# A hybrid attention and recurrence block on one core: buffers of the recurrence moved out of the merge's memory, score matmuls reshaped, and stores moved to GpSimd

## The chip, the cores and the metric

The kernel runs on one core of one Trainium2 chip, in one launch. The core has a matrix engine (TensorE, PE), a vector engine (VectorE, DVE), an activation engine (ScalarE, ACT), a general engine (GpSimd, POOL) and an engine that mostly issues transfers (SyncE, SP). Each engine works through its own instructions in order, and waits at an instruction for semaphores that other engines and transfers raise. The metric is the device time of one execution in microseconds (us); lower is better. Everything is computed in fp32.

## The reference

The input x is 1024 positions by 1024 channels. It is normalised, and one input projection gives everything that two branches need. Branch A is dilated window attention with three groups of eight heads; branch B is a gated linear recurrence in both directions with eight heads.

```python
ATTN_GROUPS = ((128, 1), (512, 4), (2048, 16))     # (window, dilation)
...
def dilated_window_attention(q, k, v, bias_table, window, dilation):
    side = (window // 2) // dilation
    blk = side
...
    s = jnp.einsum('bnqrhd,bnkrhd->bnrhqk', qb, kh) + bias
    s = jnp.where(valid[None, :, None, None], s, NEG_INF)
    m = jnp.max(s, axis=-1, keepdims=True)
    p = jnp.exp(s - m)
...
def hgrn2_scan(q, i, z_f, lb):
    f = lb + (1.0 - lb) * jax.nn.sigmoid(z_f)
    return gla_chunk_scan(q, 1.0 - f, i, jnp.log(f))
```

A block of 64 queries sees the keys of its own block and of the block on each side (its halo), as far as these exist; keys outside the window or the sequence are masked. The three groups' outputs are merged per head, weighted by their softmax denominators. In the recurrence, the logarithms of the gate f are summed along each chunk, and q and k are scaled by exponentials of those sums. Each branch is multiplied by its gate and projected; the two are merged by sigmoid gates, pass an output projection and are added to x.

## The kernel before, in words

The work runs in stages, told here by the profiled run's times. Until about 684 us PE does the largest products of the input projection (each fp32 product as three products of high and low parts: tiles whi, wlo, hh, hl). From 684 to 850 comes attention, with the products for the recurrence's values (psum tiles gp) filling PE between attention's steps. From 850 to 925 the groups' outputs are merged (tiles og, macc, gal), beside products for the recurrence's q and f. From 925 to 1233 comes the recurrence, and then the end projections.

The order of instructions isn't written by hand. A planner (classes Plan and Builder) keeps a model clock for each engine; tasks have dependencies and a priority, and `tick` and `burst` place them when the model says that their inputs are there and the buffers are free. Matmuls of attention are placed between units of gp products. `Ring` is a set of buffers used in turn: a buffer is handed out again once its last use is done. All instructions are recorded by one helper at line 58, so that tiles name them.

Attention handles a pair of blocks of 128 positions at a time, for four heads (a pair is given by group g, half hv and first block i0). `scores` (from line 1340) puts query times key into psum tiles sc, two for each block (j = 0, 1). In group 0, a block u takes 4 matmuls of 128 keys, the block's own, and then small ones of 64 queries by 64 keys for the halos (`halo(g, i)`): keys to the left for the first 64 queries (e = 0), keys to the right for the other 64 (e = 1). The halos share columns 128 to 191. At the two ends of the sequence there is no halo on one side; that corner (64 partitions by 2 x 64) is set to NEG by a memset on DVE ahead of the matmuls. In group 1 a block takes 4 matmuls of 192 keys; in group 2 only matmuls of 64 by 64. Behind the matmuls DVE adds the bias and takes the maximum of each row (`as<-sc,abias`), ACT exponentiates (`as<-as,neg`), PE transposes (pT), DVE and ACT copy out (apt), and `pv` multiplies by the values (o); DVE and ACT copy one half each of the result into one of two buffers aos, and `keep_o` (line 1490) stores it to DRAM, oD, by SP. `evac_early` (line 1640) copies a finished gp product into a buffer `stage` and stores it to ibD, by SP too, through `store` (line 653).

SBUF is given out in pools that open and close. The merge's pool "merge" closes when the merge's last store (oaD<-macc) is placed, and pool "hgrn2" opens on the same memory, so whatever first writes a tile of "hgrn2" waits for the merge's last users of that memory. Pool "hgrn" had been opened earlier, on other memory. The recurrence's first head goes: sigmoid of sk and logarithm qr<-sk on ACT (`logs`), the running sum Bc on DVE (`sums`), copies mm on POOL, differences qr and q_0 on DVE, exponentials km, qr and q on ACT, decays G (`decay`), then sk times G on DVE and the transposes kT on PE. Before, all of these tiles but sk lie in "hgrn2".

## Time and profile before

| | |
|---|---|
| times of three runs | 1441.4, 1436.46, 1439.83 us |
| median | 1439.83 us |
| the profiled execution's own time | 1438.22 us |
| its span, first to last instruction | 1436.4 us |
| mean granted clock of TensorE | 0.996 |
| TensorE busy | 1416.6 us, 99% of the span |
| VectorE, ScalarE, GpSimd busy | 67%, 61%, 24% |

A row of the timeline gives start, duration, engine, line, operation, output<-inputs, shapes, and how many like it stand in a row; in brackets is the idle time of the engine just before it and what ended it. A row on PE in which many matmuls stand together counts each matmul in two records. PEclk is the granted clock as a share of full speed. "SPq" and "POOLq" are transfers issued by those engines.

### The profile page before, as it was taken

The numbers are of one execution on the slowest core, as the hardware profiler recorded it, in microseconds if no ns is written. First come the engines' busy times: TensorE is split into PE (matmuls) and PEld (weight loads), VectorE is DVE, ScalarE is ACT, GpSimd is POOL, SyncE is SP. The second block draws the span as 40 slices with busy tenths as digits, with TensorE's granted clock in tenths as the row PEclk, the third lists the DMA queues.
The fourth block names the chain that finished last, engine by engine and source line by source line (L and its number), as shares of the span: only waits on it lengthen the run. The fifth ranks groups of instructions, "written<-read, shape, count | busy, mean of one in ns | idle before, by whom it ended". The sixth has DMA issues, their size and how long they took to land. (4 is left out here: it accounts for less than half of the span.)

```text
span 1436.4 us, 24409 instructions
## 1 busy us (share of the span) xinstructions
PE 1416.6 (99%) x8666; PEld 1177.1 (82%) x8666; DVE 962.4 (67%) x1935; ACT 875.2 (61%) x1879; POOL 338.4 (24%) x340
## 2 busy tenths in 40 slices
PE   9999999999999999999899999989999999999998
PEld 7788888888888888888778788878888888787887
DVE  6673677778675788431356657886888786358973
ACT  7743667566574766444577643576878684558461
POOL 0102334455433433334020000031222221001011
PEclk9999999999999999999999999999999999999999
DMA  7856567776733354423887329755444453778665
GB/s 239 183 140 193 169 200 168 186 160 154 173 118 104 80 119 113 129 104 118 273 280 245 118 71 273 212 122 125 116 105 127 103 153 84 226 227 218 186 162 137
DMA packets 231862, 230.32 MB, mean 160 GB/s; under 512 B 74755, under 2 KB 157979, under 8 KB 231228
## 3 DMA queue, kind: packets, MB, share of 16 engines
q1 hardware_dynamic: 217052, 203.41, 46.7%
q0 software_dynamic: 13824, 25.17, 11.5%
q8 instruction: 68, 1.11, 0.3%
q14 instruction: 54, 0.44, 0.1%
q10 hardware_dynamic: 864, 0.19, 0.1%
HBM read 168.77 MB, written 81.43 MB: 174 GB/s over the span
## 5 line engine op out<-in xcount | busy, mean ns | idle before, releaser
L58 POOL TENSOR_TENSOR wlo<-qraw,whi 128x512 fp32r<-128x512 f32 x135 | 194.2, 1444 | 378.1 <-ACT whi L58 287.8
L58 ACT ACTIVATE whi<-qraw 128x512 fp32r<-128x512 f32 x189 | 117.5, 626 | 100.9 <-DVE qraw L58 42.5
L58 DVE TENSOR_TENSOR qraw<-qraw,qraw 128x512 f32<-128x512 f32 x108 | 96.3, 892 | 40.5 <-POOL wlo L58 25.3
L58 PE MATMUL gp<-hh,whi 128*128 128x512 f32 x264 | 109.5, 415 | 0.0
L58 PE MATMUL gp<-hh,wlo 128*128 128x512 f32 x264 | 103.7, 393 | 0.0
L58 PE MATMUL gp<-hl,whi 128*128 128x512 f32 x264 | 103.1, 390 | 0.0
L58 ACT ACTIVATE whi<-raw 128x512 fp32r<-128x512 f32 x92 | 57.6, 627 | 60.4 <-DMA raw<-in_w_in_dram 31.6
L58 ACT ACTIVATE as<-as,neg 128x192 f32<-128x192 f32 (+1 forms) x192 | 77.7, 408 | 21.5 <-DVE neg L58 21.5
L58 PE MATMUL qA<-hh,whi 128*128 128x512 f32 x216 | 84.0, 389 | 0.0
L58 PE MATMUL qA<-hl,whi 128*128 128x512 f32 x216 | 84.0, 389 | 0.0
L58 PE MATMUL qA<-hh,wlo 128*128 128x512 f32 x216 | 84.0, 389 | 0.0
L58 POOL COPY mm<-Bc 128x8 f32<-128x8 f32 x64 | 32.6, 541 | 204.3 <-DVE Bc L58 126.0
L58 PE MATMUL gp<-whi,hh 128*128 128x512 f32 x192 | 79.1, 412 | 1.0 <-ACT stage L58 1.0
L58 PE MATMUL gp<-wlo,hh 128*128 128x512 f32 x192 | 75.2, 392 | 0.4 <-DVE wlo L58 0.4
L58 PE MATMUL gp<-whi,hl 128*128 128x512 f32 x192 | 75.1, 391 | 0.0
L58 DVE TENSOR_TENSOR wlo<-qraw,whi 128x512 fp32r<-128x512 f32 x54 | 37.3, 691 | 51.6 <-ACT whi L58 50.9
L58 ACT ACTIVATE ny<-ny 128x512 f32<-128x512 f32 x96 | 60.8, 633 | 5.2 <-DMA qkD<-ny 1.5
L58 DVE SCALAR_TENSOR_TENSOR ny<-ny,spare 128x512 f32<-128x512 f32 x48 | 62.3, 1298 | 1.6
L58 DVE CUSTOM_DVE_ANT_0 as<-sc,abias 128x192 f32<-128x192 f32 (+1 forms) x192 | 48.5, 308 | 21.8 <-PE sc L58 20.7
L58 PEld LDWEIGHTS gp<-hh,wlo 128*128 128x128 f32 x264 | 49.5, 188 | 11.0
L58 POOL DMA_DIRECT2D wlo<-in_w_in_dram x36 | 31.6, 877 | 113.9 <-ACT wlo L58 91.0
L58 PEld LDWEIGHTS gp<-hh,whi 128*128 128x128 f32 x264 | 49.8, 189 | 8.5
(307 smaller groups left out, 4150.7 us busy)
## 6 DMA issues: line engine op xcount, KB each, us to landing
qraw<-in_w_in_dram SPq DMA_DIRECT2D x108, 256.0 KB, 3.3
raw<-in_w_in_dram SPq DMA_DIRECT2D x84, 256.0 KB, 3.4
qkD<-ny SPq DMA_DIRECT2D x48, 256.0 KB, 3.3
wlo<-in_w_in_dram POOLq DMA_DIRECT2D x36, 256.0 KB, 4.3
sg<-sgD SPq DMA_DIRECT2D x32, 256.0 KB, 3.3
eraw<-wsD SPq DMA_DIRECT2D x32, 256.0 KB, 3.1
sgD<-stage SPq DMA_DIRECT2D x26, 256.0 KB, 2.7
ak<-qkD SPq DMA_DIRECT2D x6, 1024.0 KB, 7.5
```

Of the source, the lines that this page charges most:

```text
L58: got = f(*args, **kw)
```

## The change

It has four parts, which the planner then places anew.

First, the rings qr, q2, mm and G and the tiles Bc and Gt, which the recurrence's first head writes first, are made in pool "hgrn", ahead of the merge's end, and no longer in "hgrn2". The ring km, the loads ig and the others stay in "hgrn2".

Second, in `scores` the memsets of the masked corners stand behind all matmuls of the pair.

Third, the block's own matmuls in group 0 are 192 keys wide, the block's 128 and the 64 to its right, so the right halo of the second 64 queries needs no small matmul. In the first 64 queries the 64 columns to the right are overwritten: by the small matmuls of their left halo, or, in block 0, by the memset. The last block stays at 128 wide. All wide matmuls of both blocks come first, then the small ones.

Fourth, attention's output stores oD go by GpSimd, and the ibD stores too, while attention runs.

```diff
-    def store(dst, t, parts=None):
+    def store(dst, t, parts=None, eng="sp"):
...
-            s_.dma_start(dst, t.rearrange("p (a c) -> p a c", a=parts) if parts else t)
+            (g_ if eng == "pool" else s_).dma_start(dst, t.rearrange("p (a c) -> p a c", a=parts) if parts else t)
...
-        b.task("sp", [t], f, 1)
+        b.task(eng, [t], f, 1)
...
+        parts, blank = [], []
         for u in range(2):
             i = i0 + u
...
-            for e in range(2):
-                if g == 0 and e not in [x[0] for x in part]:
-                    for j in range(2):
-                        v_.memset(pss[u][j][64 * e:64 * e + 64, :, 128:192], NEG)
...
+            k0, n, some = ((128 * i, 192, [x for x in halo(0, i) if x[0] == 0 or i == 7]),
+                           (256 * (i // 2) + 64 * u, 192, ()), (0, 0, [(e, 2 * i + e) for e in range(2)]))[g]
+            if g == 0:
+                n = min(n, S - k0)
+                blank += [(u, e) for e in range(2) if (i, e) in ((0, 0), (7, 1))]
+            parts += [(u, e, x) for e, x in some]
...
+        for u, e in blank:
+            for j in range(2):
+                v_.memset(pss[u][j][64 * e:64 * e + 64, :, 128:192], NEG)
...
-            s_.dma_start(oD[g, 2 * hv:2 * hv + 2, :, 128 * i0:128 * i0 + 256].rearrange("a p q -> p a q"),
+            g_.dma_start(oD[g, 2 * hv:2 * hv + 2, :, 128 * i0:128 * i0 + 256].rearrange("a p q -> p a q"),
...
-        b.task("sp", [os], out, 1)
+        b.task("pool", [os], out, 1)
...
-            store(ibD[pr, i], t)
+            store(ibD[pr, i], t, eng="pool" if att else "sp")
...
     sk_ring = b.ring(hp, "sk", 7, [128, 512])
+    qr_ring = b.ring(hp, "qr", 8, [128, 512])
+    q2_ring = b.ring(hp, "q2", 6, [128, 4, 64])
+    mm_ring = b.ring(hp, "mm", 4, [128, 3, 8])
+    G_ring = b.ring(hp, "G", 4, [128, 8, 2])
+    sums_pool = hp
...
-    qr_ring = b.ring(hp, "qr", 8, [128, 512])
-    q2_ring = b.ring(hp, "q2", 6, [128, 4, 64])
...
-    mm_ring = b.ring(hp, "mm", 4, [128, 3, 8])
-    G_ring = b.ring(hp, "G", 4, [128, 8, 2])
...
-        Bc = hp.tile([128, 512], F32, tag="Bc", name=b.name("Bc"), bufs=2)
+        Bc = sums_pool.tile([128, 512], F32, tag="Bc", name=b.name("Bc"), bufs=2)
...
-        t = hp.tile([128, 8], F32, tag="Gt", name=b.name("Gt"), bufs=2)
+        t = sums_pool.tile([128, 8], F32, tag="Gt", name=b.name("Gt"), bufs=2)
```

The first place is ACT at the start of the recurrence: four sigmoids, a table load, the logarithms qr, the copy of the next f product (sk<-gp), and the first exponential km. In brackets stand the semaphores waited for (DMAHW: transfers, DVE, Activation, PE: those engines). Before:

```order
L58 ACTIVATE sk_9403<-sk_9403 128x512
L58 ACT_TABLE_LOAD
L58 ACTIVATE qr_9514<-sk_9293,lbv,omlb 128x512 [waits DMAHW3_49,DMAHW4_49,DMAHW2_49,DMAHW5_49,DMAHW1_49,DMAHW7_49,DVE_49,Activation_49]
L58 ACTIVATE qr_9516<-sk_9361,lbv,omlb 128x512 [waits Activation_49]
L58 ACTIVATE sk_9556<-gp_9476 128x512 [waits PE_49]
L58 ACTIVATE km_9558<-qr_9514,lomlb 128x4x64 [waits DVE_49,Activation_49]
```

And now:

```order
L58 ACTIVATE sk_9347<-sk_9347 128x512
L58 ACT_TABLE_LOAD
L58 ACTIVATE qr_9458<-sk_9237,lbv,omlb 128x512 [waits Activation_49]
L58 ACTIVATE qr_9460<-sk_9305,lbv,omlb 128x512 [waits Activation_49]
L58 ACTIVATE sk_9500<-gp_9420 128x512 [waits PE_49]
L58 ACTIVATE km_9502<-qr_9458,lomlb 128x4x64 [waits DMAHW3_49,DMAHW4_49,DMAHW2_49,DMAHW5_49,DMAHW0_49,DMAHW6_49,DVE_49,Activation_49]
```

The wait for the merge's transfers has moved from the first qr to the first km; the order of the instructions is the same.

The second place is PE at a pair of blocks at the start of the sequence in group 0 (sc_7836 and sc_7837 are block 0, sc_7838 and sc_7839 block 1). Before:

```order
L58 MATMUL sc_7836<-ak_7400,aq_7475 128x128 [waits DMAHW4_49,DMAHW6_49,DVE_49,PE_49]
L58 MATMUL sc_7837<-ak_7400,aq_7475 128x128 [waits DVE_49,PE_49]
L58 MATMUL sc_7836<-ak_7400,aq_7475 128x128
L58 MATMUL sc_7837<-ak_7400,aq_7475 128x128
L58 MATMUL sc_7836<-ak_7400,aq_7475 64x64
L58 MATMUL sc_7837<-ak_7400,aq_7475 64x64
L58 MATMUL sc_7836<-ak_7400,aq_7475 64x64
L58 MATMUL sc_7837<-ak_7400,aq_7475 64x64
L58 MATMUL sc_7838<-ak_7400,aq_7475 128x128 [waits Activation_49]
L58 MATMUL sc_7839<-ak_7400,aq_7475 128x128 [waits PE_49]
```

And now:

```order
L58 MATMUL sc_7836<-ak_7400,aq_7475 128x192 [waits DMAHW4_49,DMAHW3_49,DVE_49]
L58 MATMUL sc_7837<-ak_7400,aq_7475 128x192 [waits DVE_49]
L58 MATMUL sc_7836<-ak_7400,aq_7475 128x192
L58 MATMUL sc_7837<-ak_7400,aq_7475 128x192
L58 MATMUL sc_7838<-ak_7400,aq_7475 128x192 [waits Activation_49]
L58 MATMUL sc_7839<-ak_7400,aq_7475 128x192 [waits DVE_49,PE_49]
L58 MATMUL sc_7838<-ak_7400,aq_7475 128x192
L58 MATMUL sc_7839<-ak_7400,aq_7475 128x192
L58 MATMUL sc_7838<-ak_7400,aq_7475 64x64
L58 MATMUL sc_7839<-ak_7400,aq_7475 64x64
L58 MATMUL sc_7838<-ak_7400,aq_7475 64x64
L58 MATMUL sc_7839<-ak_7400,aq_7475 64x64
```

DVE's semaphore stood for the memsets at the first matmul before, and stands for earlier copies now; 12 small matmuls of this pair became 4, and they come last. In the whole program PE's instructions go from 6598 rows to 6542.

The third place is POOL in the middle of attention. Before, its row from the last wlo of attention goes straight on to `L58 MEMSET mx`, and these stores stood on SP, between loads of keys, queries and values:

```order
L58 DMA ak_7400<-qkD 128x2x1024 [waits DMAHW4_49,PE_49]
L58 DMA oD<-aos_7439 128x2x256 [waits DMAHW5_49,DVE_49,Activation_49]
L58 DMA aq_7475<-qkD 128x2x1024 [waits DMAHW6_49]
L58 DMA oD<-aos_7518 128x2x256 [waits DMAHW7_49,DVE_49,Activation_49]
L58 DMA av_7550<-vD 128x256 [waits DMAHW0_49,PE_49]
```

On POOL there now stands:

```order
L58 DMA oD<-aos_7247 128x2x256 [waits DMASW0_49,DVE_49,Activation_49]
L58 TENSOR_TENSOR wlo_7258<-raw_7107,whi_7257 128x512 [waits DMAHW6_49,PE_49,Activation_49]
L58 DMA oD<-aos_7300 128x2x256 [waits DMASW1_49,DVE_49,Activation_49]
L58 DMA oD<-aos_7439 128x2x256 [waits DMASW2_49,DVE_49,Activation_49]
L58 DMA oD<-aos_7518 128x2x256 [waits DMASW3_49,DVE_49,Activation_49]
L58 DMA oD<-aos_7584 128x2x256 [waits DMASW4_49,DVE_49,Activation_49]
```

24 stores of oD and 15 of ibD have gone from SP (785 rows before, 746 now) to POOL (344 before, 383 now). The loads on SP keep their order and no longer stand behind a store that waits for DVE and ACT.

## The prediction

> **What bounds the kernel now.** I read the page's busy table first, then the chain that ended last, then what PE waited for, and at each of those waits the timeline. One execution was profiled: span 1436.4 us, time 1438.22 us, so 1.8 us lie around the span. The median of the three runs, 1439.83, is 1.6 us above it. I make the sum against 1438.2 and add 1.6 at the end. Busy time and counts by engine:

> ```profile
> PE 1416.6 (99%) x8666; PEld 1177.1 (82%) x8666; DVE 962.4 (67%) x1935; ACT 875.2 (61%) x1879; POOL 338.4 (24%) x340
> ```

> PE is idle for 1436.4 - 1416.6 = 19.8 us only. An edit on another engine can win no more than a part of that, or clock that PE lost by standing still. What PE waited for (total us, times, longest):

> ```profile
> PE kT L58 <- DVE sk L58: 5.0, 1, 5.0
> PE sc L58 <- DMA av<-vD: 2.6, 1, 2.6
> ...
> PE sc L58 <- DVE sc L58: 1.0, 1, 1.0
> PE sc L58 <- PE o L58: 0.9, 1, 0.9
> ```

> The change aims at three of these rows: the 5.0 (recurrence's start), the 1.0 and the 0.9 (scores). None of them has an output store as releaser. The granted clock in one-microsecond steps around the two long stalls (columns: window, length, PE busy, granted clock, DMA share, GB/s) shows that a stall costs more than itself:

> ```profile
> 698.00:699.00 1.00, 1.00 (x51) 0.50 0.80 236
> 701.00:702.00 1.00, 1.00 (x6) 1.00 0.83 287
> 817.00:818.00 1.00, 0.47 (x28) 1.00 0.00 0
> 936.00:937.00 1.00, 0.00 (x0) 0.60 0.99 383
> 942.00:943.00 1.00, 1.00 (x6) 0.50 0.09 18
> 943.00:944.00 1.00, 1.00 (x6) 0.99 0.06 16
> ```

> After the 2.6 us stall before 697 the clock is half until about 700.7; after the 5.0 us stall until 943.0. Work from 939.03 to 943.0 at half speed loses about 2.0 us; the first stall loses about 1.7. The 1.0 us stall at 817 lost no clock. [...]

> **The change part by part.** *Tiles of the recurrence outside the merge's memory.* The chain that releases the 5.0 us row:

> ```profile
> 924.49 0.68 DVE L58 TENSOR_TENSOR wlo<-raw,whi 128x512 fp32r<-128x512 f32 x1
> 924.60 0.32 SPq L58 DMA_DIRECT2D oaD<-macc  x1
> 926.92 2.94 ACT L58 ACTIVATE qr<-sk,lbv,omlb 128x512 f32<-128x512 f32 x4 [4.59 <-DMA oaD<-macc]
> 927.82 1.23 DVE L58 TENSOR_TENSOR_SCAN Bc<-rst,qr 128x512 f32<-128x512 bf16 x1 [2.65 <-ACT qr L58]
> 930.24 0.50 ACT L58 ACTIVATE km<-qr,lomlb 128x256 f32<-128x256 f32 x1
> 938.20 1.16 DVE L58 TENSOR_TENSOR sk<-km,G 128x512 f32<-128x512 f32 x2
> 939.03 1.09 PE L58 MATMUL kT<-ident,sk 128*128 128x128 f32 x4 [4.99 <-DVE sk L58]
> ```

> ACT's logarithm qr stands idle 4.59 us until the merge's last store (issued 924.60) has landed, because qr's buffer lies in memory that the merge still holds. With its own buffer, qr is ready to run at 922.33, takes about 0.7 (2.94 for four), and is done by 923.1. But the scan behind it runs on DVE, which is on the merge's last operations and then wlo until 924.49 + 0.68 = 925.17. DVE's idle time before the scan is 2.65 us, so the scan can start about 2.63 us earlier (925.19 for 927.82), not 4.59. From there DVE works without a break to sk, so sk and kT follow 2.63 earlier, if ACT's km, which still lies in the merge's memory, keeps pace: released at about 926.6 to 926.9, needed at 930.24 - 2.63 = 927.6. It does, by about 0.7 us. The stall becomes 4.99 - 2.63 = 2.36 us: **-2.6**. If ACT or POOL (copies of the scan's sums) is late by that margin the term falls to -1.6; it cannot exceed -4.6.

> The clock: a 2.36 us stall lies under the 2.6 that lost it and above the 1.0 that did not. If it is lost for one spell of 3.4 us, as at 697 to 700.7, there is 1.7 of loss for 2.0, a gain of 0.3; if it is kept, 2.0. Where the stall falls against the clock's own grid decides (both spells here are 3.41 us or twice that); I take **-0.8**, between the two and nearer to the row of 2.6. [...]

> *Masked corner behind the scores.* Four pairs of blocks at the sequence's ends set a corner of the scores to minus infinity before PE may write the rest:

> ```profile
> 788.27 0.31 DVE L58 MEMSET sc<- 64x128 f32 x2
> 788.54 2.28 PE L58 MATMUL sc<-ak,aq 64*128 64x128 f32 x40 [0.93 <-PE o L58]
> 818.45 2.23 PE L58 MATMUL sc<-ak,aq 64*128 64x128 f32 x40 [0.97 <-DVE sc L58]
> ```

> The releaser of the first is named as PE's own o, but PE starts at 788.54 as the two memsets end (788.27 + 0.31), so both stalls are the same wait. PE's first matmul no longer waits for them: **-1.9** (0.93 + 0.97). The other two pairs show no stall. The memsets (0.31 us a pair) now stand on DVE ahead of the masked maximum, hidden as long as PE has gp rows of the projection to do, as it does behind every scores group. If PE had to wait for them, 4 x 0.31 = 1.2 would come back; bounds -1.9 and -0.7.

> *Scores 192 wide.* A pair of blocks in the middle was 8 matmuls of 128 and 16 of 64; it is now 8 of 192 and 8 of 64. Rows for each, with what follows on PE:

> ```profile
> 793.81 2.14 PE L58 MATMUL sc<-ak,aq 64*128 64x128 f32 x48
> 795.89 0.50 PE L58 MATMUL gp<-whi,hh 128*128 128x512 f32 x1
> 775.44 1.57 PE L58 MATMUL sc<-ak,aq 64*128 64x192 f32 x16
> 776.94 0.50 PE L58 MATMUL gp<-whi,hh 128*128 128x512 f32 x1
> 715.20 1.24 PE L58 MATMUL sc<-ak,aq 64*64 64x64 f32 x64
> 716.37 0.50 PE L58 MATMUL gp<-whi,hbh 128*128 128x512 f32 x1
> ```

> The old pair takes 795.89 - 793.81 = 2.08. Eight of 192 take 776.94 - 775.44 = 1.50. Thirty-two of 64, which fill all four quarters of the array, take 1.17, so sixteen 0.58 and eight 0.29. But the eight that remain all write one half of the partitions, so they use two quarters, and then cost as much as sixteen: the old pairs of x40, with twelve small matmuls, take no less than those of x48 (788.54 to 790.75, where a gp row starts, is 2.21). So the new pair costs 1.50 + 0.29 = 1.79 to 1.50 + 0.58 = 2.08: nothing to -0.3 for each of the four middle pairs, and -0.1 to -0.5 for the four at the ends, which have four small ones at the start of the sequence. Summed: -0.4 to -3.2. Since no row shows wide matmuls with half-filled ones behind them, and changing between forms may cost something (0.1 a pair at most, by the rows that differ 2.08 to 2.21), I take **-0.5** and keep +1.0 to -3.2 as bounds. In return all eight wide ones now run ahead of the first block's small ones, so the first block is ready after 1.50 and its small ones rather than after half of 2.08: its maximum starts some 0.6 us later in each pair. PE has gp rows there; I price what shows through at **+0.3** of 8 x 0.6 = 4.8, bounds 0 and +2.

> *Stores by GpSimd.* 24 stores of attention's output and 14 or 15 of the recurrence's values (256 KB each) leave SP's queue for POOL's, which carries wlo loads of 256 KB already:

> ```profile
> wlo<-in_w_in_dram POOLq DMA_DIRECT2D x36, 256.0 KB, 4.3
> sgD<-stage SPq DMA_DIRECT2D x26, 256.0 KB, 2.7
> L58 POOL DMA_DIRECT2D wlo<-in_w_in_dram x36 | 31.6, 877 | 113.9 <-ACT wlo L58 91.0
> 852.63 1.90 DVE L58 TENSOR_TENSOR sel<-ident 128x512 fp32r<-128x512 f32 x3 [2.62 <-DMA oD<-aos]
> 857.22 0.69 DVE L58 TENSOR_TENSOR wlo<-raw,whi 128x512 fp32r<-128x512 f32 x1 [2.70 <-ACT whi L58]
> 722.98 0.38 ACT L58 ACTIVATE aos<-o 128x256 f32<-128x256 f32 x1 [0.28 <-ACT as L58]
> 730.60 0.42 DVE L58 COPY aos<-o 128x256 f32<-128x256 f32 x1
> 726.99 0.36 ACT L58 ACTIVATE aos<-o 128x256 f32<-128x256 f32 x1
> 732.75 0.38 ACT L58 ACTIVATE aos<-o 128x256 f32<-128x256 f32 x1
> ```

> Each costs POOL about 0.88 us to issue (38 x 0.88 = 33 us, and POOL is 24% busy), and lands about 4.3 us later where an SP store takes 2.7. No PE wait above ends with such a store, and SP, whose loads stood behind them, held PE up only once (the 2.6). So the removal gains nothing. The lateness is hidden: attention has two output buffers (filled half by DVE, half by ACT), and a buffer is free from the end of one copy to the next copy but one: 723.36 to 730.60 is 7.2 us, the usual distance at its shortest, and 727.35 to 732.75 the tightest I found, 5.4, against 0.88 + 4.3 = 5.2. At the end the merge's sel, which waits for the last store, comes about 0.9 - 0.3 + 4.3 - 2.7 = 2.2 us later, while DVE then has 2.70 us free before its next row. So **0**, bounds 0 and +1 (one copy late by a us). One store of 256 KB now runs at about 690.6 rather than 699.3, in the stretch where DMA is the reason for the 2.6 us stall; 256 KB at the 370 GB/s of that stretch is 0.7 us. I take **+0.3**, bounds 0 and +0.7. [...]

> Sum: -2.6 - 0.8 - 1.9 - 0.5 + 0.3 + 0.3 = -5.2. On the profiled run 1433.0; on the median **1434.6**.

> **The rivals.** *Clock kept and halos overlapped.* The 2.36 us stall loses no clock (-1.2 more, for 2.0 instead of 0.8), and eight small matmuls cost near 0.29 (-1.5 more): 1434.6 - 2.7 = 1431.9. For it: the stall is shorter than both that lost clock. Against: 2.36 is close to 2.6. [...]

> *Given back.* The stall keeps its clock loss (+0.5), the late maximum shows through (+1.5) and the memsets cost a part of their gain (+0.8): 1434.6 + 2.8 = 1437.4, within 0.3%. For it: attention's chain scores, maximum, exponential, transposes has DVE on it, and DVE gets both the later start and the blanks. Against: PE waits in attention are few though DVE is often late already.

> *The memory was not the bound.* qr was released by DMA, but if km (still in the merge's memory) or POOL's copies end last, the start moves by only 1 us: 1434.6 + 1.6, and the clock's 0.8 goes too: 1437.0. For it: a margin of only 0.7 us.

> *Stores that hold up the output buffers (slower).* Each of the 24 output stores goes into a POOL queue in order, behind wlo of 1.44 us or a store that itself waits:

> ```profile
> DMA to landing us min/median/max: 2.1/3.0/6.1
> L58 POOL TENSOR_TENSOR wlo<-qraw,whi 128x512 fp32r<-128x512 f32 x135 | 194.2, 1444 | 378.1 <-ACT whi L58 287.8
> ```

> The worst SP landing was 6.1; on POOL with 1.44 ahead and 0.88 of issue that is 8.4 us, over the 7.2 until the buffer is needed. If each of the 24 held its copy by 8.4 - 7.2 = 1.2 and half of that reached PE, it would be 24 x 0.6 = 14: 1434.6 + 14 = 1448.6. It decides from a landing above 7.2 - 0.88 = 6.3 us, or 4.9 behind a wlo. Against: medians of 3.0 and 4.3, and PE's gp rows as cover.

> **How the numbers follow.** A measurement of this kernel tells about 0.3%, 4.3 us, from no change; the three runs spread over 4.9. Forecast 0.45, clock and halos 0.18, given back or memory not the bound 0.28, stores 0.09. The forecast's own uncertainty (the median's noise is about 1.5) lets some quarter of its cases end above 1435.5, the bound for faster. So faster is 0.45 x 0.75 + 0.17 + 0.28 x 0.15 = 0.55; slower (above 1444.1) is 0.06 of the stores' 0.09 and 0.01 of the rest, 0.07; the same 0.38 is what is left. The range reaches from the better rival, 1431.9, to the given-back one, 1437.4, each widened by half the spread of the three runs, 2.5: 1429.5 to 1440.0.

> **What would show it.** In the profile after: qr's idle time ends by itself or not at all, the scan begins right behind wlo, kT's wait is 2.4 (1.6 to 3.4); the two rows of 1.0 and 0.9 are gone; a middle pair takes 1.8 to 2.1; stores of oD on POOL's queue land in 4 to 5, and no PE row names aos or oD. The prediction is wrong if kT's wait is still above 4, if a new PE wait in attention names DVE's maximum or ACT's aos, or if the clock shows half in further places.

## The result and the profile after

| | before | changed |
|---|---|---|
| median | 1440.16 us (5 runs, 1436.46 to 1441.4) | 1430.15 us (5 runs, 1429.77 to 1432.59) |
| ratio, 95% interval | | 0.9937 [0.9921, 0.9953] |
| the profiled execution: span, mean granted clock | 1436.4 us, 0.996 | 1428.4 us, 1.000 |

The kernel is 0.63% faster, 10.0 us by the medians and 8.0 by the spans of the two profiled executions. That is the side forecast and within the range, near its lower end (1429.5), but nearly twice the sum of 5.2 us. The page's busy line of the changed kernel, and what PE waits for now:

```profile
PE 1412.8 (99%) x8554; PEld 1174.9 (82%) x8554; DVE 960.1 (67%) x1935; ACT 874.0 (61%) x1879; POOL 363.0 (25%) x379
```

```profile
PE sc L58 <- DMA av<-vD: 3.1, 1, 3.1
PE al L58 <- DVE og L58: 2.3, 2, 1.4
PE warm L58 <- DVE warm L58: 1.4, 1, 1.4
PE gp L58 <- issue: 1.4, 1, 1.4
PE kT L58 <- DVE sk L58: 1.4, 1, 1.4
```

PE is idle 1428.4 - 1412.8 = 15.6 us where it was 19.8. The two memset rows are gone and kT's wait is 1.4, not 5.0 and not the 2.4 that was forecast. A wait of 2.3 for the merge (al) stands where 0.2 stood. The other 3.8 us are less busy time: a matmul at half clock counts as busy for longer (in the kernel before, gp matmuls follow each other every 0.43 us at half clock, from 940.77, and every 0.23 at full, from 943.31), so clock that is won back shows there, and the score matmuls became shorter. The chain at the recurrence's start, on the timeline of the changed kernel:

```profile
920.81 2.93 ACT L58 ACTIVATE qr<-sk,lbv,omlb 128x512 f32<-128x512 f32 x4
922.09 0.68 DVE L58 TENSOR_TENSOR wlo<-raw,whi 128x512 fp32r<-128x512 f32 x1
922.21 0.32 SPq L58 DMA_DIRECT2D oaD<-macc  x1
922.69 1.22 DVE L58 TENSOR_TENSOR_SCAN Bc<-rst,qr 128x512 f32<-128x512 bf16 x1
924.72 0.51 ACT L58 ACTIVATE km<-qr,lomlb 128x256 f32<-128x256 f32 x1 [0.50 <-DVE qr L58]
933.04 1.15 DVE L58 TENSOR_TENSOR sk<-km,G 128x512 f32<-128x512 f32 x2
933.87 0.63 PE L58 MATMUL kT<-ident,sk 128*128 128x128 f32 x4 [1.36 <-DVE sk L58]
```

This is as forecast: qr has no idle time in brackets, and the scan starts right behind wlo. From the last oaD store to the scan it was 927.82 - 924.60 = 3.2 us and is 0.5. Four kT matmuls took 1.09 us and take 0.63: they run at full clock now. Granted clock at the changed kernel's two stalls (window, length, PE busy, clock, DMA share, GB/s):

```profile
697.00:698.00 1.00, 0.40 (x23) 1.00 0.34 108
698.00:699.00 1.00, 1.00 (x83) 1.00 0.59 184
...
933.00:934.00 1.00, 0.13 (x1) 1.00 0.86 274
934.00:935.00 1.00, 1.00 (x7) 1.00 0.91 309
```

Neither stall lost the clock in this execution, not even the 3.1 us one at attention's start, where a stall of 2.6 us cost the kernel before 1.7 us. A pair of blocks of group 0 at the sequence's start and one in the middle, each with the matmul that follows:

```profile
786.22 1.95 PE L58 MATMUL sc<-ak,aq 64*128 64x192 f32 x24
788.10 0.50 PE L58 MATMUL gp<-whi,hh 128*128 128x512 f32 x1
791.15 2.18 PE L58 MATMUL sc<-ak,aq 64*128 64x192 f32 x32
793.26 0.50 PE L58 MATMUL gp<-whi,hh 128*128 128x512 f32 x1
```

The middle pair takes 2.11 (2.08 before): the eight small matmuls cost as much as sixteen. The pair at the start takes 1.88 (2.21 before). Over the eight pairs that is 16.0 us for 16.9.

### The profile page after: what moved, and what is told of

Same layout as the page of the kernel before. It is cut to its first block, busy times and chain, and to the rows that moved or that the text cites. A ratio compares the mean times of both kernels' runs of the same rounds, so it can differ in the third digit from the quotient of the medians.

```text
span 1428.4 us, 24200 instructions
## 1 busy us (share of the span) xinstructions
PE 1412.8 (99%) x8554; PEld 1174.9 (82%) x8554; DVE 960.1 (67%) x1935; ACT 874.0 (61%) x1879; POOL 363.0 (25%) x379
## 5 line engine op out<-in xcount | busy, mean ns | idle before, releaser
L58 POOL TENSOR_TENSOR wlo<-qraw,whi 128x512 fp32r<-128x512 f32 x135 | 194.1, 1443 | 378.4 <-ACT whi L58 297.4
L58 ACT ACTIVATE whi<-qraw 128x512 fp32r<-128x512 f32 x189 | 117.8, 627 | 99.7 <-DVE qraw L58 40.9
L58 DVE TENSOR_TENSOR qraw<-qraw,qraw 128x512 f32<-128x512 f32 x108 | 95.9, 889 | 38.9 <-POOL wlo L58 28.1
L58 PE MATMUL gp<-hh,whi 128*128 128x512 f32 x264 | 109.5, 415 | 0.0
L58 PE MATMUL gp<-hh,wlo 128*128 128x512 f32 x264 | 103.7, 393 | 0.0
L58 PE MATMUL gp<-hl,whi 128*128 128x512 f32 x264 | 103.0, 390 | 0.0
L58 ACT ACTIVATE whi<-raw 128x512 fp32r<-128x512 f32 x92 | 57.6, 627 | 60.6 <-DMA raw<-in_w_in_dram 32.5
L58 ACT ACTIVATE as<-as,neg 128x192 f32<-128x192 f32 (+1 forms) x192 | 77.8, 411 | 24.9 <-DVE neg L58 24.8
L58 PE MATMUL qA<-hh,whi 128*128 128x512 f32 x216 | 84.0, 389 | 0.0
L58 PE MATMUL qA<-hl,whi 128*128 128x512 f32 x216 | 84.0, 389 | 0.0
L58 PE MATMUL qA<-hh,wlo 128*128 128x512 f32 x216 | 84.0, 389 | 0.0
L58 POOL COPY mm<-Bc 128x8 f32<-128x8 f32 x64 | 32.7, 542 | 189.2 <-DVE Bc L58 185.5
L58 PE MATMUL gp<-whi,hh 128*128 128x512 f32 x192 | 79.1, 412 | 0.0
L58 PE MATMUL gp<-wlo,hh 128*128 128x512 f32 x192 | 75.2, 392 | 0.3 <-DVE wlo L58 0.3
L58 PE MATMUL gp<-whi,hl 128*128 128x512 f32 x192 | 75.1, 391 | 0.0
L58 DVE TENSOR_TENSOR wlo<-qraw,whi 128x512 fp32r<-128x512 f32 x54 | 37.3, 691 | 50.8 <-ACT whi L58 50.8
L58 ACT ACTIVATE ny<-ny 128x512 f32<-128x512 f32 x96 | 60.8, 633 | 5.2 <-DMA qkD<-ny 1.5
L58 DVE CUSTOM_DVE_ANT_0 as<-sc,abias 128x192 f32<-128x192 f32 (+1 forms) x192 | 48.4, 308 | 21.3 <-PE sc L58 20.3
L58 DVE SCALAR_TENSOR_TENSOR ny<-ny,spare 128x512 f32<-128x512 f32 x48 | 60.9, 1268 | 1.7
L58 POOL DMA_DIRECT2D wlo<-in_w_in_dram x36 | 31.1, 864 | 112.1 <-ACT wlo L58 84.7
L58 PEld LDWEIGHTS gp<-hh,wlo 128*128 128x128 f32 x264 | 49.5, 188 | 11.1
L58 PEld LDWEIGHTS gp<-hh,whi 128*128 128x128 f32 x264 | 49.7, 188 | 8.5
## 6 DMA issues: line engine op xcount, KB each, us to landing
qraw<-in_w_in_dram SPq DMA_DIRECT2D x108, 256.0 KB, 3.4
raw<-in_w_in_dram SPq DMA_DIRECT2D x84, 256.0 KB, 3.3
qkD<-ny SPq DMA_DIRECT2D x48, 256.0 KB, 3.1
wlo<-in_w_in_dram POOLq DMA_DIRECT2D x36, 256.0 KB, 4.3
sg<-sgD SPq DMA_DIRECT2D x32, 256.0 KB, 2.7
eraw<-wsD SPq DMA_DIRECT2D x32, 256.0 KB, 2.8
sgD<-stage SPq DMA_DIRECT2D x26, 256.0 KB, 2.7
```

What stands on the lines that cost most here:

```text
L58: got = f(*args, **kw)
```

## The experiments

Eight of the kernels are the change taken apart, in the two directions; two fill PE's idle time; two look for a better version. All ratios are to the kernel before on the same chip.

**The memory alone.** Only the rings and tiles moved, as in the change's last lines:

```diff
     sk_ring = b.ring(hp, "sk", 7, [128, 512])
+    qr_ring = b.ring(hp, "qr", 8, [128, 512])
+    q2_ring = b.ring(hp, "q2", 6, [128, 4, 64])
+    mm_ring = b.ring(hp, "mm", 4, [128, 3, 8])
+    G_ring = b.ring(hp, "G", 4, [128, 8, 2])
+    sums_pool = hp
```

> The kernel before with the first part alone: rings qr, q2, mm, G and tiles Bc, Gt out of the merge's memory. Sum of the forecast: the wait of kT falls from 5.0 to 2.4 us and the clock gives 0 to 2.0 more, so 2.6 to 4.6 us faster than before (ratio 0.9968 to 0.9982). Rival, the merge's end decides alone: the profile of the changed kernel shows the merge's last store 2.4 us earlier, and if that and not the memory moved the start, this part alone gives under 1 us and kT's wait stays at 4 or more.

Measured: 1437.41 us, ratio 0.9976 [0.9965, 0.9988], so 3.5 us faster, within the 2.6 to 4.6 forecast; kT's wait is 3.2, not 2.4. In this execution the merge's last store fell later (926.27), yet the scan began 0.5 us behind it, as in the changed kernel. The rival falls.

**The stores alone**, oD and ibD by GpSimd:

```diff
-            s_.dma_start(oD[g, 2 * hv:2 * hv + 2, :, 128 * i0:128 * i0 + 256].rearrange("a p q -> p a q"),
+            g_.dma_start(oD[g, 2 * hv:2 * hv + 2, :, 128 * i0:128 * i0 + 256].rearrange("a p q -> p a q"),
...
-            store(ibD[pr, i], t)
+            store(ibD[pr, i], t, eng="pool" if att else "sp")
```

> The kernel before with the stores by GpSimd alone. Forecast: nothing, or 0.3 us slower. Rival read from the two traces: SP's loads of weights come free of the stores that wait for DVE and ACT, so ACT's wait of 2.44 us for raw at 744 falls under 1 and PE's wait of 1.0 for ACT's stage at 752 goes; 1 to 2 us faster by the end of attention, against which stands a wait of about 2 us of ACT for the landing of an output store near 717, which costs PE under 1.

Measured: 1438.71 us, 0.9992 [0.998, 1.0004]. In the time it can't be told from nothing. The trace shows both halves of the rival. Before and changed, the same row of ACT in attention:

```profile
746.86 0.63 ACT L58 ACTIVATE whi<-raw 128x512 fp32r<-128x512 f32 x1 [2.44 <-DMA raw<-in_w_in_dram]
```

```profile
745.16 0.63 ACT L58 ACTIVATE whi<-raw 128x512 fp32r<-128x512 f32 x1 [0.71 <-POOL wlo L58]
```

A weight load that stood on SP behind a store, which itself waited for ACT, now comes in time. Against it stand, in the changed kernel, this row and two of DVE, which waited 2.68 us at 717.13 and 2.09 at 726.71 for the same cause:

```profile
717.11 0.39 ACT L58 ACTIVATE aos<-o 128x256 f32<-128x256 f32 x1 [2.39 <-DMA oD<-aos]
```

This is the forecast's "one copy late": an output buffer waits for its store to land. By 741.9 the changed kernel's scores are again where they were before (741.91 and 741.87), after having been 1 us ahead at 707; so what was won at attention's start was lost by there.

**Both score parts, without the rest.**

```diff
+            k0, n, some = ((128 * i, 192, [x for x in halo(0, i) if x[0] == 0 or i == 7]),
...
+        for u, e in blank:
+            for j in range(2):
+                v_.memset(pss[u][j][64 * e:64 * e + 64, :, 128:192], NEG)
```

> The kernel before with both changes in the scores (192 wide, corner behind). Forecast: 1.9 for the two memset waits and 0.5 for the matmuls, 2.4 us faster at the end of attention and at the end of the kernel. Rival, the merge takes it back: the merge waits for its own loads, PE comes early and stands at the al products or longer at kT, and of 2.4 to 2.9 gained by 862 less than half is left at the end.

Measured: 1437.29 us, 0.9984 [0.9972, 0.9996]: 2.3 us by the ratio, at the forecast's 2.4. The profile shows the rival's mechanism: kT waits longer than before.

```profile
PE kT L58 <- DVE sk L58: 5.6, 1, 5.6
PE sc L58 <- DMA av<-vD: 3.3, 1, 3.3
```

PE came earlier and stood longer, and in that one execution hardly anything was left (span 1436.2). The times of the twelve runs say that in the middle more is.

**The memsets behind the matmuls, nothing else.**

```diff
-            for e in range(2):
-                if g == 0 and e not in [x[0] for x in part]:
-                    for j in range(2):
-                        v_.memset(pss[u][j][64 * e:64 * e + 64, :, 128:192], NEG)
+            blank += [(u, e) for e in range(2) if g == 0 and e not in [x[0] for x in part]]
```

> The kernel before with the memsets of the masked corner behind the matmuls and nothing else. Forecast: the waits of 0.93 and 0.97 us go, 1.9 us faster by the end of attention. Rival: under 1 at the end of the kernel, since the merge's loads hold the recurrence's start where it was.

Measured: 1432.56 us, 0.9949 [0.9932, 0.9967]. That is 7 us for 8 memsets, against 1.9 forecast, and more than both score parts together. Both expectations are wrong. PE's waits in its profile:

```profile
PE al L58 <- DVE og L58: 2.5, 1, 2.5
PE sc L58 <- DMA av<-vD: 2.4, 1, 2.4
PE warm L58 <- DVE warm L58: 1.4, 1, 1.4
```

There is no row for kT at all. The planner had made another order of the same instructions on PE, in attention and after it: of the projection's matmuls (gp), 690 stand ahead of attention's last product where 696 stood before, and 1050 ahead of the first kT where 1038 stood. What that order does is told with the last experiment but one. This profile is of the slowest of the six runs.

**One store.** Only the last ibD store ahead of the merge's first loads goes by GpSimd:

```diff
+            store(ibD[pr, i], t, eng="pool" if (pr, i) == (1, 5) else "sp")
```

> The kernel before with one instruction moved: the last ibD store of attention's end (waited for ACT's stage until 855.76 in the kernel before, ahead of the merge's first loads nst on SP) goes by GpSimd; PE's order is unchanged. Theory, the merge starts when SP comes free: nst loads start near 853 instead of 856.31, the merge's last store and the scan move 2 to 3 us, kT's start 2.6 us, and this one store gives as much at the recurrence as all 39 in the stores-alone run; 1.5 to 3 us faster than before. Forecast's view, stores cost and gain nothing: within 0.5 us of before.

Measured: 1438.44 us, 0.9988 [0.9972, 1.0003]. Before, and in this run:

```profile
856.31 2.37 SPq L58 DMA_DIRECT2D nst<-stD  x4
```

```profile
852.95 2.62 SPq L58 DMA_DIRECT2D nst<-stD  x4
...
938.31 1.09 PE L58 MATMUL kT<-ident,sk 128*128 128x128 f32 x4 [4.17 <-DVE sk L58]
```

The loads start 3.4 us earlier, as expected, but kT only 0.7 earlier (939.03 before). By the trace the theory that SP's queue at this place sets the recurrence's start falls: the merge gives most of it back on its way. The times alone, 1.7 us faster with an interval from 0.4 slower to 4.0, don't decide it.

**The change without the stores, and without the memory.** In each, that part is taken back to what it was before.

> The changed kernel with all stores back on SP. Forecast (stores nothing): within 0.5 us of the changed kernel, 9 to 10 us faster than before. Theory that time is set by the release of kT through the merge: 2.6 us of the changed kernel's gain are lost, nst loads start near 855, scan 2.6 us earlier than before relative to the merge's end and not more, kT's wait 2.5 to 3.5 us; 1433 to 1436.

Measured: 1431.37 us, 0.9938 [0.9919, 0.9957]: the changed kernel's ratio. The forecast's view holds, and the theory of the release through the merge falls again.

```profile
PE sc L58 <- DMA av<-vD: 2.4, 1, 2.4
PE al L58 <- DVE og L58: 1.9, 1, 1.9
PE kT L58 <- DVE sk L58: 1.4, 1, 1.4
```

> The changed kernel with the recurrence's tiles back in the merge's memory. Forecast: 3.4 us lost of the changed kernel's gain, of it 2.6 in kT's wait. Theory of the release: kT starts about 2.6 us earlier than in the kernel before (the merge's start) and PE, which arrives some 1.5 to 3 us earlier, waits 4 to 5 us, so nothing of the scores' gain survives: 1436 to 1438.

Measured: 1435.48 us, 0.997 [0.996, 0.998]: 5 us of the changed kernel's gain lost, where the forecast had 3.4, and a little faster than the theory's 1436 to 1438. kT waits 5.2 us, as the theory had it within a little:

```profile
PE kT L58 <- DVE sk L58: 5.2, 1, 5.2
PE pT L58 <- issue: 2.1, 1, 2.1
```

**The oD stores alone back on SP.**

```diff
-            g_.dma_start(oD[g, 2 * hv:2 * hv + 2, :, 128 * i0:128 * i0 + 256].rearrange("a p q -> p a q"),
+            s_.dma_start(oD[g, 2 * hv:2 * hv + 2, :, 128 * i0:128 * i0 + 256].rearrange("a p q -> p a q"),
```

> The changed kernel with the 24 output stores oD back on SP and the ibD stores by GpSimd. Theory: the merge's start stays early (nst near 853), ACT's wait of 2.39 us for an output buffer near 717 goes, but SP's weight loads stand behind oD stores again (ACT's wait for raw at 744 back to about 2.4); within 1.5 us of the changed kernel. Rival, that the oD stores carry the gain: 2 us or more slower than the changed kernel.

Measured: 1431.49 us, 0.9939 [0.9926, 0.9953]: no difference to the changed kernel that these runs resolve. ACT's wait for an output buffer is gone and its wait for raw is back (2.5 us): a trade of equals. This execution has kT's wait at 2.0 us and shows what that does to the clock:

```profile
932.00:933.00 1.00, 0.01 (x1) 1.00 0.86 291
933.00:934.00 1.00, 0.00 (x0) 1.00 0.83 215
934.00:935.00 1.00, 0.96 (x5) 0.52 0.93 262
...
936.00:937.00 1.00, 1.00 (x3) 0.50 1.09 305
937.00:938.00 1.00, 1.00 (x6) 0.78 1.09 234
```

One spell of about 3.4 us at half clock, all of it on work.

**PE's idle time filled** with matmuls on a constant, whose output the real ones overwrite; in the kernel before (12 and 23 of them) and in the changed one (14 and 6):

```diff
         ps = bank("kT")
+        if k_next[0] == 1:
+            for _ in range(23):
+                t_.real.matmul(ps[:, 0:128], ident, ident, start=True, stop=True)
```

> The kernel before with idle PE time filled: 12 matmuls of 128x128 on a constant ahead of attention's first scores and 23 ahead of the first kT, into psum that the real ones then overwrite, so that PE stands still only briefly where it stood 2.6 and 5.0 us; nothing is released earlier. Theory, the clock is its own term: granted clock 0.999 to 1.000 in every run where before's runs have 0.995 to 0.999, and 2 to 4 us faster than before with the same start of kT in the profile. Rival, the half clock costs nothing since the next wait takes it back: same time as before, or slower where the filler runs past the release.

Measured: 1438.05 us, 0.9989 [0.9978, 1.0]; mean clock over its runs 0.9996, where before's 15 runs beside it have 0.9973. So the clock does come back. The time is some 1.6 us shorter, at the edge of what these runs resolve and less than the 2 to 4 expected, although nothing was released earlier and the filler ran 1.4 us past the release in the profiled execution (its row begins at 937.67, the first kT follows it at 942.80, while a scan at 930.19 releases kT 11.2 us later, at 941.4).

> The changed kernel with the same filler, 14 matmuls ahead of attention's first scores and 6 ahead of the first kT. Theory: the changed kernel has already won the clock at kT; what its runs still lose (0.997 to 1.000) is lost at the first scores; clock 0.999 or more, 0.5 to 2 us faster than the changed kernel. Rival, the gain after attention's start is taken back by ACT's wait for an output buffer near 717: no change.

Measured: 1432.07 us, 0.9954 [0.9942, 0.9967]: no gain, rather a loss. Fourteen matmuls took 3.29 us and held the first scores until 698.77, 1.2 us later than without, and the granted clock of its runs (mean 0.9988) is no better than the changed kernel's 0.9986. The theory's half on this kernel falls. The trace shows why the clock was no better: both places kept it, and the one spell at half clock (886.25 to 889.66) follows a stall of 2.35 us in the merge, at al, which no filler covered. The profiled run of the other filled kernel lost its only spell in the same way (2.30 us at al, half clock from 890.86).

**The changed kernel with 128-wide matmuls**, so that of the scores only the memsets move, in the order that the planner made for that:

> The changed kernel with group 0's own matmuls 128 wide and its small ones as before, the memsets still behind. PE's order is then that of the run with the corner alone, which differs from before's in attention and after it and showed no wait at kT. Forecast: 0.5 us slower than the changed kernel (the matmuls cost 16.9 us in place of 16.0 in the two traces, and the order changes nothing). Rival, the order decides: with kT's wait gone and the merge started early, 2 to 4 us faster than the changed kernel.

Measured: 1427.37 us (1427.02 to 1430.93), 0.9926 [0.9913, 0.9939]. The forecast's view, 0.5 us slower, falls; the intervals of this kernel and the changed one overlap, so that it is faster than the changed one is likely, not shown. Attention's last values, the merge's first loads and the first transposes:

```profile
841.02 1.45 PE L58 MATMUL o<-apt,av 64*64 64x128 f32 x56
...
846.43 3.08 SPq L58 DMA_DIRECT2D nst<-stD  x4
...
932.39 0.60 PE L58 MATMUL kT<-ident,sk 128*128 128x128 f32 x4
```

Attention ends at 842.5, in the changed kernel at 848.8 and before at 849.4. Of the 6.4 us to the changed kernel, 2.1 already stand at attention's first scores (695.54 for 697.60, behind a wait for av of 1.0 for 3.1 us, which differs from execution to execution). For the other 4.3 the lists of PE say why: ahead of attention's last product there stand 696 matmuls of the projection (gp) before, 711 in the changed kernel and 690 here. At 0.23 us from one to the next, 21 more are 4.8 us. So what the changed kernel saves in attention the planner filled with more of the gp products, which are due at any time, and attention's end hardly moved forward. Here the merge's loads start 6.4 us earlier than in the changed kernel, the scan at 919.04 for 922.69, and kT waits for nothing.

That kT waits for nothing does not come from the early start, though. The run with the corner alone has exactly this order on PE, and its first kT came later than in the kernel before (939.03), again without a wait:

```profile
940.73 0.60 PE L58 MATMUL kT<-ident,sk 128*128 128x128 f32 x4
```

In this order 360 gp matmuls stand between attention's last product and the first kT (1050 - 690), where it was 342 before and is 327 in the changed kernel: the wait is filled with work. And in these two runs the scan waits for ACT's qr (4.01 and 3.70 us), which itself does not wait for the merge's store, so the memory part has nothing left to win there.

**Three output buffers**, in that kernel:

```diff
-                            ("s", 6, [128, 3, 4, 64]), ("pt", PT, [128, 2, 2, 128]), ("os", 2, [128, 2, 2, 128]),
+                            ("s", 6, [128, 3, 4, 64]), ("pt", PT, [128, 2, 2, 128]), ("os", 3, [128, 2, 2, 128]),
```

> The run before this one (changed kernel, 128-wide matmuls, corner behind) with three output buffers of attention in place of two; PE's order is the same. Theory: ACT's wait for the landing of an oD store near 717 (2.39 us in the changed kernel) goes, attention's third group of scores starts 1 to 2 us earlier, and since attention's end starts the merge, 0.5 to 2 us faster than with two buffers: 1425.5 to 1427. Rival: the wait is covered by PE's other work or taken by the next one (ACT's stage), so no change: 1427 to 1428.

Measured: 1428.04 us, 0.9911 [0.9889, 0.9932]. ACT's wait for the buffer (1.8 us with two) is gone, and the time is the same: the rival holds, that wait was covered.

## Why the prediction was right, and where its sizes were off

The side and the cause at the recurrence were right. The size is another matter: 1430.15 lies below even the better rival's 1431.9, and the range holds it only because both ends were widened by half the spread of three runs. In the two profiled executions the 8.0 us are 4.2 of idle time and 3.8 of busy time. Of the idle time kT gives 3.6 and the memset rows 1.9, the merge takes 2.1 and the first scores 0.5; smaller rows make up the rest. Of the busy time about 1.9 is clock at kT, 0.9 the score matmuls, and 1.7 clock at attention's start, which is luck, as shown below; 0.7 goes the other way elsewhere. Of the terms:

- **Memory, -2.6 in kT's wait.** The distance from the merge's last store to the scan is 3.2 us in the profiles without this part (before, the stores alone, the scores alone, the change without the memory) and 0.5 in those with it (the changed kernel, the memory alone, the change without the stores, the oD stores on SP): 2.7 us, as the step "about 2.63 us earlier, not 4.59" had it. In the changed kernel the wait fell by 3.6, since DVE's end of the merge also moved 2.4 us forward (wlo from 924.49 to 922.09) and PE's arrival only 1.5 (it stood 2.3 us in the merge). The term was right for the memory and left out that second shift.
- **The clock, -0.8: mis-sized.** The step took a residual stall of 2.36 us and put it between a stall that lost the clock and one that did not. The stall came out at 1.4, below the 1.6 to 3.4 that was to show the forecast, and under every one at this place that lost it: 2.0 lost one spell, 3.2, 4.0, 4.2, 5.0, 5.2 and 5.6 lost two (6.8 us, in part idle), 1.4 lost none, in the changed kernel and in the one without the stores. First kT to first U (the recurrence's next matmuls) is 944.47 - 939.03 = 5.44 us before and 937.44 - 933.87 = 3.57 after: 1.9 us, near the upper bound of 2.0. In the profiles that have this wait, it came to 2.0 or less only with memory and scores together. The mean granted clock over the runs shows the memory's share and does not separate the rest: before 0.9972, scores alone 0.9968, the changed kernel without the memory 0.9968; memory alone 0.9985, the changed kernel 0.9986, with its oD stores on SP 0.9984, without any of its stores 0.9997. The parts alone, -3.5, -1.2 and -2.3 us by their ratios, sum to 7.0, not to the 9 that the whole ratio gives; with intervals of some 1.7 us on each this is a hint and no proof.
- **Memsets, -1.9.** The two rows went. Their own price can't be read from the run that moved them alone, because the planner's order changed with them.
- **192 wide, -0.5.** The matmuls alone give -0.9. But an assumption under the sum, that the new order around the scores costs and gains nothing, failed: the list was known to be placed anew, and what it does to attention's end (15 more gp matmuls ahead of it, 3.4 us) and to the stretch behind it (15 fewer) stood in the order and was not counted. In the order without this part the same other parts give a time at least as good, and the memsets alone give 7.3 us.
- **Late maximum +0.3, loads +0.3.** No PE row names the maximum. The first stall is 3.1 for 2.6, but it is 0.3 to 3.3 across the runs, so a difference of 0.5 says nothing.
- **Stores, 0.** Right within what these runs resolve (alone 0.9992 [0.998, 1.0004]; the change without them 0.9938). The tight place at two buffers was real: stores of oD landed in 3.7 us at the median but in up to 8.5, past the 6.3 from which the slower rival was to decide; ACT waited 2.4 us there and DVE 2.7, and no row of PE names it. Alone, it cost nothing that could be measured.

The length of a stall alone does not sort the runs: 2.0 us lost the clock at kT (the oD stores on SP), 2.4 lost it at attention's start (the corner alone, the change without the stores), and 3.1 and 3.3 there did not (the changed kernel, the scores alone). The spells last 3.4 us or twice that.

The idle time within steps read off the traces does sort them. Within each profiled execution all changes of the granted clock lie a whole number of steps of 3.413 us apart (in the kernel before 697.27, 700.68, 936.20 and 943.03, that is 0, 1, 70 and 72 steps). With steps of that length laid on from those changes (in the changed kernel from the first record of full clock, 6.26 us, 201 steps ahead of 692.34), PE's idle time within each can be read. In the fourteen traces, from 20 us after the start to 5 us before the end, all 15 steps at full clock with 1.98 us or more of idle time were followed by half clock, and none with 1.92 us or less was:

| run | step of 3.413 us | PE idle in it, us | clock in the next step |
|---|---|---|---|
| kernel before, first scores | 693.86 to 697.27 | 2.54 | half |
| kernel before, kT | 932.79 to 936.20 | 2.16 | half |
| changed kernel, first scores | 692.34 to 695.75 | 1.25 | full |
| changed kernel, first scores | 695.75 to 699.17 | 1.85 | full |
| scores alone, first scores | 695.81 to 699.22 | 1.92 | full |
| without the memory, pT in attention | 721.22 to 724.63 | 1.98 | half |
| oD stores on SP, kT | 930.62 to 934.03 | 2.03 | half |
| change without the stores, first scores | 695.74 to 699.15 | 2.36 | half |

So the 3.1 us stall kept the clock by luck, where an edge between two steps parted it into 1.25 and 1.85, while a stall of 1.4 us is shorter than every idle time here that was followed by half clock, wherever the edges fall: by these numbers the clock at kT is the change's own gain. The 2.36 us stall of the prediction would have lost its clock in something over half of the positions, an estimate from these numbers with 1.95 as the middle of 1.92 and 1.98, (3.41 + 2.36 - 2 x 1.95) / 3.41 = 0.55. So for a stall of that length a value between the two was fair; what was wrong was the length. The two numbers are read off traces whose ends of matmuls are modelled, and no run moved a stall along the steps.

What stays open: why the merge takes back 2.7 of the 3.4 us by which its loads start earlier with one store moved. In the kernel before its transfers keep the DMA engines busy (a share of 1.00 to 1.12 in steps of 10 us from 861 to 911), but no run took any of them away.

## What to carry to other kernels

Where the critical engine fills its waits with work that is due at any time, read where a change lets that filler go: a stage in front ends sooner only if the saved time isn't given to filler, and a wait behind it goes when enough filler is left for it. Counting the filler ahead of the stage's last instruction, and from there to the wait, tells both without a run. Price a stall with the clock that it loses, and ask which parts together bring it under the length that lost it: here 1.98 us of idle time within one step of 3.413 us. A buffer whose memory is held by the stage before cost the time from when the next engine was free anyway (here DVE) to when the stage's last store let it go on, 2.7 us, and nothing in the order in which ACT was later still.

## What the runs showed of the hardware

Eight small 64x64 matmuls that all write the same half of the partitions, behind eight wide ones, took 0.6 us in the changed kernel (2.11 - 1.50), half of the 1.2 us that thirty-two over both halves took in the kernel before (715.20 to 716.37). In the changed kernel a GpSimd store of 256 KB took 0.57 us (ibD) or 0.72 us (oD) to issue, less than the 0.86 of its weight loads, and 39 of them added 25 us to GpSimd's busy time; with them ACT waited 2.4 us and DVE up to 2.7 us for an output buffer, at 717 and 726.7.
